# Block 2's mixers: the delta rule's chains as a third chain beside the RWKV column tiles

## The chip, the cores and the metric

The kernel runs on one core of a Trainium2 chip. The metric is the device time of one execution in microseconds (us). TensorE is called PE, VectorE DVE, ScalarE ACT, GpSimd POOL, and SyncE, which issues most DMAs, SP.

## What is computed

The program runs two blocks over 256 tokens of width 1024: a first block with its own mixers and a large expert layer, then a second block. Only the second block's mixing sublayer is touched. It projects the normalised input by `w_in`, splits the columns into a part for a gated delta rule (4 heads of 128), a part for RWKV-7 (8 heads of 64) and two gates, runs both recurrences in both directions over the sequence, and merges them:

```python
def gated_delta_chunked(q, k, v, g, beta, s0):
    ...
    gc = jnp.cumsum(g, axis=-1)
    a_mat = jnp.eye(CHUNK_2, dtype=jnp.float32) + lower
    sol = lax.linalg.triangular_solve(a_mat, rhs, left_side=True, lower=True, unit_diagonal=True)
    ...
    def step(s, inp):
        u_c, w_c, qk_c, qd_c, kd_c, ge_c = inp
        v_new = u_c - jnp.einsum('...ck,...kv->...cv', w_c, s)
        o_c = jnp.einsum('...ck,...kv->...cv', qd_c, s) + jnp.einsum('...ij,...jv->...iv', qk_c, v_new)
        s = s * ge_c[..., None, None] + jnp.einsum('...ck,...cv->...kv', kd_c, v_new)
        return s, o_c

def rwkv7_scan(r, w, k, v, a, b, s0):
    def step(s, inp):
        r_t, w_t, k_t, v_t, a_t, b_t = inp
        sa = jnp.einsum('...vk,...k->...v', s, a_t)
        s = s * w_t[..., None, :] + sa[..., :, None] * b_t[..., None, :] + v_t[..., :, None] * k_t[..., None, :]
        return s, jnp.einsum('...vk,...k->...v', s, r_t)

def merge_branches(gates, o_a, o_b, w_o_a, w_o_b, w_out):
    g_a, g_b = jnp.split(gates, 2, axis=-1)
    y = jax.nn.sigmoid(g_a) * (o_a @ w_o_a) + jax.nn.sigmoid(g_b) * (o_b @ w_o_b)
    return y @ w_out
```

## The kernel before

**RWKV.** The 512 channels are cut into four column tiles j of two heads each. A tile has a front, two backs and an output. `rwkv_front` makes, for each direction, the scaled operands and eight products `rmt` (L1648) that DVE and ACT evacuate into masks and transposes. `rwkv_back` is one chain per direction: an inverse (`mixed_inverse`: eight small tiled products `r0ic` or `r1ic` of L1172, then `ib` and `iy` of L1200, each of which needs the evacuated one before) and then four recurrence steps over chunks, each with the products L1681 (state by key), L1696 (inverse by residual) and L1703 (update), with an ACT or DVE evacuation between them; L1711 and L1688 add into the output. `rwkv_out` normalises (`ryt`, L1747, and `rgb`, L1752). The two directions go step by step in turn, with PSUM banks of their own (tags `pa` and `pc`), in `in_turn`.

**The delta rule.** It has four chains: two head pairs hp by two directions d. A chain takes the products of its head pair (`gdn_products`), a decay mask (`grb`, then DVE and ACT work on `gdec` and `gN`), an inverse with the prefix `gi`, and two recurrence steps (`gp`). It is written behind all RWKV tiles, in `gdn`: the two chains of hp 0 one after the other, those of hp 1 in step with each other from a second pool X.

**Work in queues.** Products that wait for nothing but their weights stand in two queues of generators. `waiting[0]` holds the next RWKV tile's preparation, `ahead(j+1)`: its projections (36 steps with the small ones), then `rn`, `rvb` and `rbw` (L1563, L1572, L1587) on the one bank of tag `pd`. `waiting[1]` holds the projections of head pair 1, the gate `gz` (L1856) and 16 early merge gates `early_gate` (eight `pc` products of L1110 each). `fill` takes a few steps from them behind a product of direction 0's chain. How many, by kind of product, is in `HOPS`: its entry 2 is for the inverse, 3 to 5 for the recurrence (queue 0, queue 1), and before also 6 and 7 for the delta rule.

**What sets the order.** The written order is not the order on the engines: a static scheduler puts each engine's instructions in a row when the program is built, and may move a chain's products ahead of ones written earlier. Memory pools are reused by tile, so a load may wait for the last reader of the tile that lay there before. `merge` (L1891) loads `w_o_b` in two halves on SP; ACT (L290) and DVE (L291) split each in two before the products `mo` (L300) may start.

Of the kernel before, what the change touches and what calls it, by code (L numbers as in the profile page):

```python
# [57 lines left out]

HOPS = 4, 1, (3, 1), (2, 1), (2, 1), (2, 1), (0, 4), (0, 4)
LBANKS = dict(pa=2, pc=2, pd=1, pb=2, pe=1)  # L60
# [80 lines left out]
def drain(steps):  # L141
    for _ in steps:
        pass


def run(steps):

    while True:
        try:
            next(steps)  # L150
        except StopIteration as end:
            return end.value
# [11 lines left out]
class Net:  # L164
# [796 lines left out]
    def ctx_pre(self):  # L961
# [6 lines left out]
        with tc.tile_pool(name="CW", bufs=2, reuse_waits="tile") as CW, tc.tile_pool(name="C", bufs=1, reuse_waits="tile") as C:  # L968
# [22 lines left out]
            with tc.tile_pool(name="CG", bufs=1, reuse_waits="tile") as G:  # L991
                gates = yield from self.gdn_gates(G, uT)
                for hp in range(2):
                    qkv = []
                    yield from self.gdn_in(G, uT, False, hp, load, qkv)
                    x = yield from self.gdn_products(G, qkv, False)
                    for d in range(2):
                        yield from self.gdn_dir(G, d, False, 2 * hp, gates, x, self.SA, False, None)
            with tc.tile_pool(name="CR", bufs=1, reuse_waits="tile") as R:
# [259 lines left out]

    def gdn(self, W, gates, ins, S, o, X):  # L1260


        for hp in range(2):
            x = run(self.gdn_products(W, ins[hp], True))
            args = 2 * hp, gates, x, S, True, o
            if hp == 0:
                for d in range(2):
                    drain(self.gdn_dir(W, d, False, *args))
            else:

                for _ in zip(self.gdn_dir(W, 0, True, *args), self.gdn_dir(X, 1, True, *args)):
                    pass

# [66 lines left out]

    def gdn_dir(self, W, d, both, h0, gates, x, S, lat, o):

        nc = self.nc
# [5 lines left out]
        c0 = 4 * d + h0  # L1349
        hop = (lambda *steps: (lambda ins: self.fill(ins, *steps))) if both and d == 0 else lambda *steps: (lambda ins: None)  # L1350
        rb = b4("grb")
# [12 lines left out]
        nc.scalar.activation(dec, dec, AF.Exp)  # L1364
        if not lat:
            yield
        N = W.tile([P, 2, 2, P], F32, name="gN")
# [14 lines left out]
        u4 = lambda ap: ap.rearrange("p t h c -> p (t h) c")  # L1382
        yield from self.mixed_inverse(W, u4(N), 4, d, u4(Y), 7, "gi", hop(*HOPS[6]))
        sl = S[d][:, h0:h0 + 2, :]
        for step in range(2):
# [3 lines left out]
            for h in range(2):  # L1389
                ins = nc.tensor.matmul(p1[:, h, :], kd[:, t, h, :], sl[:, h, :], start=True, stop=True)  # L1390
            hop(*HOPS[7])(ins)
            if not lat:
                yield
            r = W.tile([P, 2, P], F32, name="gr")
            nc.vector.tensor_sub(r, vN[:, t], p1)
            p2 = half("gp2")
            for h in range(2):
                ins = nc.tensor.matmul(p2[:, h, :], Y[:, t, h, :], r[:, h, :], start=True, stop=True)
            hop(*HOPS[7])(ins)
            if not lat:  # L1400
                yield
            vn = W.tile([P, 2, P], F32, name="gvn")
            nc.vector.tensor_mul(vn, p2, be[:, t, c0:c0 + 2].unsqueeze(2).to_broadcast([P, 2, P]))
            if lat:
                p3 = half("gp3")
                for h in range(2):
                    nc.tensor.matmul(p3[:, h, :], qd[:, t, h, :], sl[:, h, :], start=True, stop=False)
                    nc.tensor.matmul(p3[:, h, :], qk[:, t, h, :], vn[:, h, :], start=False, stop=True)
                ov = o[:, t, h0 * P:(h0 + 2) * P].rearrange("p (h c) -> p h c", h=2)
                if (step if both else d) == 0:  # L1410
                    nc.scalar.copy(ov, p3)
                else:
                    nc.vector.tensor_add(ov, ov, p3)
# [9 lines left out]
    def rwkv(self, W, F, uT, S, lat, load, tags, start=None):  # L1423
# [90 lines left out]
        self.waiting[0].append((tags[2], gate()))  # L1514
        start()
        for j in range(4):
# [6 lines left out]
            bo = self.rwkv_bonus(W, j, x, fr)  # L1523
            ys = self.in_turn(tags, [self.rwkv_back(j, d, x, fr[d], env) for d in range(2)])
            self.advance(self.waiting[0], 999)
# [235 lines left out]
    def lat(self):  # L1761
        tc, nc, I = self.tc, self.nc, self.I
        h = self.acc
        with ExitStack() as outer:
            L = outer.enter_context(tc.tile_pool(name="L", bufs=1, reuse_waits="tile"))
            early = [L.tile([P, KD, 256], F32, name=f"early{i}", tag=f"exp{i}") for i in range(2)]
            with self.phase(**LBANKS):
# [30 lines left out]
                self.ob = tail[:, 2, :].rearrange("p (j t) -> p j t", j=4)  # L1798
                with tc.tile_pool(name="R", bufs=1, reuse_waits="tile") as R, tc.tile_pool(name="G", bufs=1, reuse_waits="tile") as G, ExitStack() as mix:
                    slots = [self.wslot() for _ in range(3)]  # L1800
# [8 lines left out]
                    def start():  # L1809
# [5 lines left out]
                        others += [self.early_gate(j, loads[2], uT, early) for j in range(16)]  # L1815
                        self.waiting[1].extend(("pe", gen) for gen in others)

                    self.waiting = [], []
                    with tc.tile_pool(name="RF", bufs=1, reuse_waits="tile") as RF:
                        run(self.rwkv(R, RF, uT, self.SB, True, loads[0], ("pa", "pc", "pd"), start))  # L1820
                    slots[2].extend(part[:g])
                    X = mix.enter_context(tc.tile_pool(name="X", bufs=1, reuse_waits="tile"))
                    self.ptag = "pb"
                    self.gdn(G, self.gates, qkv, self.SA, go, X)
                    self.gdn_out(G, sz, go, oa)
# [477 lines left out]
```

## Time and profile before

| | us |
|---|---|
| median of 3 runs | 2464.67 (2458.88 to 2468.92) |
| the profiled execution | 2459.26 |
| its span | 2457.4 |
| block 2's mixers in it, first `afT` to first `mo` | 1676.57 to 2112.49 |
| mean granted PE clock, share of full speed | 0.97 |

PE is busy for 2280.8 of 2457.4 us, but a busy PE is not one at full speed: the granted clock falls to half in some stretches of the mixers. To read a stretch, take two things from its row: the time in which PE was not busy, and the busy time multiplied by what the clock lacked. Together they are what the stretch lost against a PE that always had work at full clock.

### The profile page before, as it was taken

Reading aid. Unit: us, or ns where it says so; the run is one execution under the profiler, and the core shown is the slowest. Engines: PE = TensorE matmul, PEld = TensorE weight load, DVE = VectorE, ACT = ScalarE, POOL = GpSimd, SP = SyncE. Lnnn points to the kernel's source line nnn. Section 1 sums busy time; section 2 is a strip of 40 time slices with the busy share of each in tenths; the row PEclk is TensorE's granted clock in tenths of the full one; section 3 lists DMA queues with packets and bytes.
Section 4 is the critical chain, followed back from the end, with each engine's and each line's share of the span. In section 5 each row is a group of like instructions: output and inputs, shape, how many; then the busy total and the mean of one; then the engine's idle time right before and its main releaser. Section 6 shows DMA issues by size and latency. Waiting matters only on the chain. (4 is left out here: it accounts for less than half of the span.)

```text
span 2457.4 us, 45180 instructions
## 1 busy us (share of the span) xinstructions
PE 2280.8 (93%) x18736; PEld 1238.1 (50%) x18736; DVE 979.8 (40%) x2419; ACT 652.7 (27%) x1652; POOL 353.7 (14%) x627
## 2 busy tenths in 40 slices
PE   7989799999999999899999999987989989989997
PEld 6756433444444443333343333325867868865554
DVE  7735311223233133232222232215576663545545
ACT  5414111211211222111122121104444433422222
POOL 3101000000000111011011011003253431300000
PEclk9989899999999999999999999998979989999999
DMA  7637999999999999999999999994211104689995
GB/s 257 213 115 262 356 395 402 402 407 406 398 400 395 366 391 405 406 408 405 406 406 404 406 407 408 406 398 115 79 39 47 52 22 145 202 278 366 366 368 181
DMA packets 318816, 755.06 MB, mean 307 GB/s; under 512 B 12944, under 2 KB 158016, under 8 KB 315536
## 3 DMA queue, kind: packets, MB, share of 16 engines
q1 hardware_dynamic: 317104, 747.67, 81.2%
q0 software_dynamic: 1504, 4.46, 0.5%
q8 instruction: 150, 2.46, 0.4%
q14 instruction: 58, 0.48, 0.1%
HBM read 751.03 MB, written 1.05 MB: 306 GB/s over the span
## 5 line engine op out<-in xcount | busy, mean ns | idle before, releaser
L909 PE MATMUL gu<-w,xs 128*64 128x512 f32 (+1 forms) x3072 | 677.7, 569 | 22.8 <-DMA w<-in_w_up 18.6
L909 PEld LDWEIGHTS gu<-w,xs 128*64 128x64 f32 x3072 | 197.1, 137 | 326.5 <-issue 257.4
L941 PE MATMUL dn<-w,hT 128*64 128x512 f32 x1408 | 336.3, 602 | 21.4 <-DMA w<-in_w_down 20.7
L1110 PE MATMUL pc<-luT,w 128*128 128x256 f32 x688 | 177.2, 399 | 2.2 <-DMA w<-in_w_in 1.5
L941 PEld LDWEIGHTS dn<-w,hT 128*64 128x64 f32 x1408 | 88.4, 136 | 176.6 <-issue 118.2
L1110 PEld LDWEIGHTS pc<-luT,w 128*128 128x128 f32 x688 | 127.3, 195 | 19.5 <-issue 1.5
L2159 PE MATMUL egu<-w,exs 128*64 128x256 f32 x1024 | 123.2, 383 | 0.0
L2159 PEld LDWEIGHTS egu<-w,exs 128*64 128x64 f32 x1024 | 74.6, 136 | 39.4 <-issue 6.9
L1692 POOL TENSOR_SCALAR rsw<-rSU,rwc 64x64 f32<-64x64 f32 x112 | 39.6, 354 | 379.1 <-DVE rSU L1708 368.9
L919 DVE TENSOR_TENSOR hid<-hid,gu 128x512 f32<-128x512 f32 (+1 forms) x48 | 30.9, 643 | 123.4 <-ACT hid L307 123.2
L920 DVE TENSOR_TENSOR hid<-hid,gu 128x512 f32<-128x512 f32 (+1 forms) x48 | 30.8, 642 | 120.4 <-PE gu L909 120.3
L1110 PE MATMUL pc<-cuT,w 128*128 128x256 f32 x288 | 71.1, 391 | 0.0
L305 ACT ACTIVATE hid<-gu 128x512 f32<-128x512 f32 (+1 forms) x48 | 26.9, 560 | 163.6 <-PE gu L909 163.4
L2186 PE MATMUL edn<-w,ehT 128*64 128x512 f32 x256 | 67.7, 597 | 0.7 <-ACT ehT L322 0.5
L1110 PEld LDWEIGHTS pc<-cuT,w 128*128 128x128 f32 x288 | 52.1, 190 | 30.8 <-issue 20.4
L291 DVE TENSOR_TENSOR wp<-w,wp 128x1024 fp32r<-128x1024 f32 (+1 forms) x44 | 57.8, 1332 | 24.2 <-ACT wp L290 24.2
L1700 DVE COPY rSU<-rp 64x64 f32<-64x64 f32 x64 | 13.5, 214 | 134.5 <-PE rp L1696 134.2
L300 PE MATMUL pj<-uTh,wp 128*128 128x272 f32 x320 | 66.0, 299 | 0.0
L1648 PE MATMUL rmt<-rT,rBK 128*128 128x128 f32 (+1 forms) x256 | 50.9, 340 | 15.3 <-DVE rT L1635 7.3
L290 ACT CAST wp<-w 128x1024 fp32r<-128x1024 f32 (+1 forms) x48 | 55.0, 1187 | 29.8 <-DMA w<-in_w_in 17.8
L1193 DVE TENSOR_TENSOR r0iB<-r0iB,r0ic 128x128 f32<-128x128 f32 x48 | 13.6, 284 | 118.5 <-PE r0ic L1172 107.2
L958 DVE SCALAR_TENSOR_TENSOR acc<-sc,aff,acc 128x512 f32<-128x512 f32 x64 | 43.7, 744 | 37.9 <-PE sc L956 37.7
(675 smaller groups left out, 3514.5 us busy)
## 6 DMA issues: line engine op xcount, KB each, us to landing
w<-in_w_down SPq DMA_DIRECT2D x176, 1024.0 KB, 16.5
w<-in_w_gate SPq DMA_DIRECT2D x128, 1024.0 KB, 17.6
w<-in_w_up SPq DMA_DIRECT2D x128, 1024.0 KB, 18.1
w<-in_w_gate SPq DMA_DIRECT2D x64, 768.0 KB, 15.8
w<-in_w_up SPq DMA_DIRECT2D x64, 768.0 KB, 14.9
w<-in_moe_w_gate SPq DMA_DIRECT2D x32, 1024.0 KB, 13.3
w<-in_moe_w_up SPq DMA_DIRECT2D x32, 1024.0 KB, 12.3
w<-in_moe_w_down SPq DMA_DIRECT2D x32, 1024.0 KB, 11.3
```

The lines of the kernel that those rows point to most:

```text
L290: self.nc.scalar.copy(hi, src)
L291: (eng or self.nc.vector).tensor_sub(lo, src, hi)
L300: self.nc.tensor.matmul(out, a[x], b[y], start=(i == 0 and x + y == 0), stop=(i == n - 1 and x == 1))
L909: ins = nc.tensor.matmul(b[h * 64:(h + 1) * 64, :w], xs[:, k, :], ws(k, slice(h * w, (h + 1) * w)), start=(k == 0), stop=(k == KD - 1))
L919: nc.vector.tensor_mul(hid, hid, gu[0][:, :w])
L941: ins = nc.tensor.matmul(dn[0][dc * 64:(dc + 1) * 64], hT[:, j, h * 64:(h + 1) * 64], wd(h * nf + j, slice(dc * 512, (dc + 1) * 512)), sta ...
L958: nc.vector.scalar_tensor_tensor(dst, b, self.aff[:, t + 1, e:e + 1], dst, op0=ALU.mult, op1=ALU.add)
L1110: self.nc.tensor.matmul(b, w(k), uT[:, k, :], start=(k == 0), stop=(k == KD - 1))
L1648: ins = nc.tensor.matmul(b[:, i], BK[:, c0 + i, h:h + 2, :], T[:, h, c0 + i, :, :], start=True, stop=True)
L1692: nc.gpsimd.tensor_scalar(sw[r], SU[r, h, c, :], wc[r, c:c + 1], 0.0, op0=ALU.mult, op1=ALU.add)
L2159: nc.tensor.matmul(b[64 * i:64 * i + 64, x * 256:x * 256 + 256], xs[:, k, i, :], w[i](k), start=(k == 0), stop=(k == KD - 1))
L2186: nc.tensor.matmul(b[64 * i:64 * i + 64, :], hT[:, j, 64 * i:64 * i + 64], wd[i](j, cs), start=(j == 0), stop=(j == 1))
```

## The change

The delta rule's chain number j runs as a third generator of `in_turn` beside RWKV tile j (tag `pb`), so `gdn`, its pool X and its own fills go. `third(j)` first pushes queue 1 until head pair 1's projections are there (j = 2). `HOPS[0]` = 10 steps of queue 1 run ahead of the first tile; the inverse's fill goes from (3, 1) to (2, 2), the recurrence's from (2, 1) to (1, 2). `gdn_dir` now gives way at every step; whether its output is copied or added hangs on d alone. The number of instructions stays: 18736 matmul records before, and no product is added or taken away.

```diff
-HOPS = 4, 1, (3, 1), (2, 1), (2, 1), (2, 1), (0, 4), (0, 4)
+HOPS = 10, 1, (2, 2), (1, 2), (1, 2), (1, 2)
...
-    def gdn(self, W, gates, ins, S, o, X):
-        for hp in range(2):
-            x = run(self.gdn_products(W, ins[hp], True))
-            args = 2 * hp, gates, x, S, True, o
-            if hp == 0:
-                for d in range(2):
-                    drain(self.gdn_dir(W, d, False, *args))
-            else:
-                for _ in zip(self.gdn_dir(W, 0, True, *args), self.gdn_dir(X, 1, True, *args)):
-                    pass
+    def gdn_turn(self, W, j, gates, qkv, S, o, held):
+        hp, d = divmod(j, 2)
+        if d == 0:
+            held[:] = [(yield from self.gdn_products(W, qkv[hp], True))]
+        yield from self.gdn_dir(W, d, 2 * hp, gates, held[0], S, True, o)
...
-        start()
+        third = start()
+        self.advance(self.waiting[1], HOPS[0])
         for j in range(4):
...
-            ys = self.in_turn(tags, [self.rwkv_back(j, d, x, fr[d], env) for d in range(2)])
+            ys = self.in_turn((*tags[:2], "pb"), [*(self.rwkv_back(j, d, x, fr[d], env) for d in range(2)), third(j)])
...
+                        held = []
+                        def third(j):
+                            while j == 2 and len(qkv[1]) < 3:
+                                self.advance(self.waiting[1], 1)
+                            return self.gdn_turn(G, j, self.gates, qkv, self.SA, go, held)
+                        return third
...
-                    X = mix.enter_context(tc.tile_pool(name="X", bufs=1, reuse_waits="tile"))
                     self.ptag = "pb"
-                    self.gdn(G, self.gates, qkv, self.SA, go, X)
                     self.gdn_out(G, sz, go, oa)
                     self.advance(self.waiting[1], 999)
```

**Place 1, PE, the recurrence of tile 0.** Before, two RWKV chains (`rp`) follow each other here without a queued product:

```order
L1688 MATMUL rp_12842<-rSU_12131,rT_11752 64x64 x2
L1696 MATMUL rp_12861<-rP_12854,rY_12222 64x64 x2
L1681 MATMUL rp_12851<-rSU_12177,rT_11753 64x64 x2
L1711 MATMUL rp_12842<-rSU_12131,rMR_12141 64x64
L1688 MATMUL rp_12851<-rSU_12177,rT_11753 64x64 x2
L1696 MATMUL rp_12872<-rP_12865,rY_12258 64x64 x2
```

After, in the same recurrence (lines are 10 lower), projections `pc`, gate products `gz` and a delta chain's inverse stand between the steps:

```order
L1693 MATMUL rp_13145<-rSU_12158,rKt_12167 64x64 x2
L1110 MATMUL pc<-luT,w 128x256
L1851 MATMUL gz<-w,luT 128x128 x4
L1701 MATMUL rp_13121<-rSU_12158,rMR_12168 64x64
L1200 MATMUL gib<-giZ,giN 128x128 x4
L1701 MATMUL rp_13132<-rSU_12201,rMR_12211 64x64
```

The queued products and the delta chain have moved in among the steps.

**Place 2, PE, from tile 0 to tile 1.** Before, tile 1's preparation (`rn`, `rvb`, `rbw`) stands at the first steps of tile 0's recurrence:

```order
L1696 MATMUL rp_12693<-rP_12686,rY_12222 64x64 x2
L1563 MATMUL rn<-rsq,stab 128x256
L1110 MATMUL pc<-luT,w 128x256
L1354 MATMUL grb<-ctab,gg 128x128 x2
L1688 MATMUL rp_12683<-rSU_12177,rT_11753 64x64 x2
```

After, it ends behind the recurrence, with products of the delta chain (`gp`) alone between, then tile 0's output and tile 1's front:

```order
L1577 MATMUL rbw<-rlo_11702,rlora 128x256
L1577 MATMUL rbw<-rlo_11703,rlora 128x256
L1396 MATMUL gp_13268<-gvn,gdec 128x128
L1395 MATMUL gp_13268<-SA_3013,ger 128x128
L1396 MATMUL gp_13268<-gvn,gdec 128x128
L1347 MATMUL grb<-stab,gg 128x128 x4
L1737 MATMUL ryt<-ctab,rys_12918 64x64 x8
L1742 MATMUL rgb<-rsg,rg_11767 128x256
L1638 MATMUL rmt<-rT_11752,rBK_13328 128x192 x2
```

The preparation has moved behind the recurrence, and between it and the front that needs it stand only these products.

**Place 3, PE, the end of the mixers.** Before, tile 3's `ryt` and `rgb` stand amid the delta rule's last inverses, some 50 rows ahead of `mo`:

```order
L1747 MATMUL ryt<-ctab,rys_15198 64x64 x8
L1200 MATMUL gib<-giZ,giN 128x128 x4
L1200 MATMUL giy<-gY,giB 128x128 x4
L1110 MATMUL pc<-luT,w 128x256 x4
L1752 MATMUL rgb<-rsg,rg_14008 128x256
```

After, RWKV's last step is followed by sixteen queued products, the delta rule's output `got`, then `ryt`, `rgb` and `mo`:

```order
L1678 MATMUL rp_16584<-rSU_15724,rT_11753 64x64 x2
L1686 MATMUL rp_16605<-rP_16601,rY_15806 64x64 x2
L1110 MATMUL pc<-luT,w 128x256 x8
L1701 MATMUL rp_16584<-rSU_15724,rMR_15734 64x64 x2
L1872 MATMUL got<-ctab,tail 128x128 x3
L1110 MATMUL pc<-luT,w 128x256 x8
L1872 MATMUL got<-ctab,tail 128x128 x3
L1737 MATMUL ryt<-ctab,rys_16353 64x64 x8
L1872 MATMUL got<-ctab,tail 128x128 x2
L1742 MATMUL rgb<-rsg,rg_14666 128x256
L300 MATMUL mo<-mob,wp 128x256 x96
```

The mixers now end with RWKV's output. The two loads of `w_o_b` take memory whose last readers are the RWKV products L1678 and L1686 shown here, so they are issued behind them; before, their waits were for RWKV tiles read earlier.

## Rows read from the trace of the kernel before

**Rows 1.** The page's first line.

```profile
span 2457.4 us, 45180 instructions
```

**Rows 2.** Busy by stretch: window, length, PE, PEld, DVE, ACT, POOL, PEclk, DMA, GB/s.

```profile
1677.00:1720.00 43.00, 36.53 (x193) 32.89 (x191) 23.86 (x69) 21.00 (x60) 20.31 (x44) 0.86 0.31 83
1720.00:1782.00 62.00, 61.56 (x773) 50.80 (x773) 32.74 (x90) 28.52 (x81) 14.28 (x26) 0.97 0.29 78
1782.00:1818.00 36.00, 27.64 (x360) 21.08 (x359) 27.66 (x77) 20.15 (x67) 18.73 (x31) 0.76 0.18 49
1818.00:1865.00 47.00, 45.16 (x790) 34.92 (x789) 26.98 (x89) 16.16 (x50) 17.68 (x38) 0.85 0.16 42
1865.00:1898.00 33.00, 29.94 (x261) 23.51 (x260) 27.09 (x76) 19.24 (x61) 15.80 (x24) 0.90 0.16 47
1898.00:1941.00 43.00, 40.82 (x926) 34.36 (x925) 25.83 (x85) 13.70 (x48) 17.21 (x38) 0.92 0.17 45
1941.00:1970.00 29.00, 28.63 (x317) 24.64 (x316) 20.66 (x60) 16.52 (x54) 11.63 (x19) 1.00 0.18 50
1970.00:2000.00 30.00, 26.68 (x403) 21.43 (x404) 24.58 (x81) 13.81 (x46) 17.14 (x30) 0.89 0.07 19
2000.00:2061.00 61.00, 53.57 (x1080) 41.03 (x1080) 25.93 (x77) 19.08 (x66) 12.26 (x22) 0.94 0.21 54
2061.00:2104.00 43.00, 41.55 (x256) 36.70 (x251) 17.20 (x35) 18.77 (x50) 4.52 (x9) 1.00 0.48 151
```

**Rows 3.** Groups of PE by form in 1677 to 2113: busy, mean ns, idle before.

```profile
L1110 PE MATMUL pc<-luT,w 128*128 128x256 f32 x688 | 177.2, 399 | 2.2 <-DMA w<-in_w_in 1.5 <-DVE tail L1860 0.7
L1648 PE MATMUL rmt<-rT,rBK 128*128 128x192 f32 x128 | 32.5, 393 | 7.9 <-ACT rT L1637 4.4 <-ACT rKt L1655 3.5
```

**Rows 4.** The same view as rows 2, in slices of 10 us.

```profile
1710.00:1720.00 10.00, 6.46 (x23) 5.99 (x23) 9.76 (x31) 3.33 (x10) 4.79 (x7) 0.51 0.01 4
1790.00:1800.00 10.00, 4.67 (x76) 3.42 (x75) 9.64 (x27) 7.74 (x26) 7.98 (x12) 0.78 0.05 13
1800.00:1810.00 10.00, 7.48 (x122) 5.54 (x114) 9.23 (x26) 4.00 (x15) 6.71 (x12) 0.50 0.01 2
```

**Rows 5.** PE's waits in 1677 to 2113: total us, times, longest.

```profile
PE rp L1711 <- DVE rSU L1700: 5.9, 6, 2.3
PE rp L1681 <- DVE rSU L1708: 5.4, 4, 2.1
PE r1ic L1172 <- DVE r1iB L1193: 4.1, 1, 4.1
```

**Rows 6.** Timeline of PE around tile 0's front: start, us, instruction, wait before it.

```profile
1698.79 0.60 PE L1563 MATMUL rn<-rsq,stab 128*128 128x256 f32 x2
1699.22 1.03 PE L1587 MATMUL rbw<-rlo,rlora 128*128 128x256 f32 x4
1701.83 1.11 PE L1587 MATMUL rbw<-rlo,rlora 128*128 128x256 f32 x4
1711.47 2.92 PE L1648 MATMUL rmt<-rT,rBK 128*128 128x192 f32 x8 [4.41 <-ACT rT L1637]
1716.46 1.62 PE L1648 MATMUL rmt<-rT,rBK 128*128 128x192 f32 x4 [2.06 <-ACT rKt L1655]
```

**Rows 7.** Timelines of the mixers' end, SP's loads, then PE, DVE, ACT.

```profile
L1891 SPq DMA_DIRECT2D w<-in_w_o_b x2: 458/490/522, 2061.2 to 2061.8; - x2
...
2054.60 0.34 PE L1711 MATMUL rp<-rSU,rMR 128*64 128x64 f32 x4
2112.49 1.77 PE L300 MATMUL mo<-mob,wp 128*128 128x256 f32 x13
...
2065.57 0.60 DVE L1753 TENSOR_TENSOR tail<-rys,rgb 128x256 f32<-128x256 f32 x1 [0.89 <-PE rgb L1752]
2075.76 2.29 DVE L291 TENSOR_TENSOR wp<-w,wp 128x2048 fp32r<-128x2048 f32 x1
...
2099.94 1.30 ACT L290 CAST mob<-tail 128x256 fp32r<-128x256 f32 x4
2105.23 1.89 ACT L290 CAST wp<-w 128x2048 fp32r<-128x2048 f32 x1
```

## What the change was expected to do

> **What bounds the kernel now.** The change touches only block 2's mixers, 1677 to 2113 us of a span of 2457.4 [rows 1]; what follows them waits for their end, so their length is the whole effect. I read first the table of busy times by stretch, which shows what PE lost in each; then PE's waits, to see which engine ended them; then the slices of 10 us, to see whether that engine was itself full; and last the timelines around the two places where the new order looks worst.
>
> From the table [rows 2], take for each stretch the time in which PE was not busy, and its busy time multiplied by the clock it lacked. For 1782 to 1818 that is 36.0 − 27.64 = 8.4, and 27.64 × (1 − 0.76) = 6.6, together 15.0 us. The ten stretches in turn lost 11.6, 2.3, 15.0, 8.6, 6.1, 5.5, 0.4, 6.3, 10.6 and 1.5 us; the last 9 us, not in the table, lost 0.6. The 11.6 lie ahead of tile 0's first products, where the new order on PE is the old one: they stay. The other 56.9 us are all that an even feed of PE could win; the work itself, 2113 − 1720 − 56.9 = 336 us at full clock, has the same instructions before and after.
>
> The reader should see the contrast in [rows 2]. Where queued projections stand between the steps (1720 to 1782, 1941 to 1970, 2061 to 2104) PE lost 2.3 + 0.4 + 1.5 = 4.2 us in 134. Where they are missing it lost 15.0 in 36. What PE waits for in the bad stretches is mostly DVE: its copies and updates of the RWKV state (5.9 and 5.4 us) and one step of an inverse (4.1) [rows 5]. In 1790 to 1810 DVE was busy for 9.64 and 9.23 of 10 us, and the granted clock went 0.78, 0.50 [rows 4], that is half its time and more at the lower of its levels, 1.2 instead of 2.4 GHz, after PE had worked for under half of a slice. So a missing filler costs twice, first as idle time and then as clock.
>
> By the Trainium skill (TensorE: Matmul & The Clock Gate, "What's actually happening") the clock granted follows how busy PE has lately been; the 0.50 behind the slice with 4.67 us of work agrees, and by that rule a stretch that is fed wins its clock too, as the sum below assumes with or without the rule.
>
> **The change part by part.** *Nothing is removed.* Of PE, DVE, ACT and POOL the work is the same; pool X's removal and the choice of copy or add by direction move one DVE or ACT instruction of about 0.4 us each and cost nothing where PE has products queued. What moves is the delta rule's chains, from behind RWKV to a place beside each tile, and the queued products, out of the delta rule's tail into the tiles. I counted PE's instructions of the new order between its marks, priced each kind by its mean (a `pc` product is two records, 177.2 us for 688, 0.52 us for the two [rows 3]) and scaled the sum to the 336 us above. Then each stretch gets the rate of loss of the stretch of [rows 2] that it is most like:
>
> 1. Tile 0, from its front to the end of its recurrence, some 102 us of work, with `pc` or `gz` behind each step: the rate of 1720 to 1782, 2.3 on 60, gives 3.8 (bounds 3, and 8, a third of what the rate of 1818 to 1865, 8.6 on 38, would give).
> 2. Tile 0 to tile 1. The recurrence has 10 × 2 + 11 × 1 = 31 places for queue 0, and `ahead(1)` has 36 steps, so `rn`, `rvb` and `rbw` now come last and one behind another on one bank. In tile 0's own front the first `rbw` started at 1699.22 and the first `rmt` at 1711.47, 12.25 us later, and from `rn` to the last `rbw` took 1701.83 − 1698.79 = 3.0 us [rows 6]. With the last projection's own evacuation, some 1.8 us as I estimate it from ACT's and DVE's 0.4 us steps, that makes 17.1 us in which PE has about 8.8 us of products: 8.3 idle. Then the front's evacuations follow: a second wait of 2.06 us stood there in tile 0 [rows 6], and its slice from 1710 lost 10 − 6.46 × 0.51 = 6.7 us in all [rows 4]. I take 5 of these, so 13.5 (bounds 9.6, where the gate's products hide part of the evacuations, and 18). In the old order the same place was the worst stretch of all, 15.0 us.
> 3. Tile 1: its inverse is fed, 45 us of work at (2.3 + 0.4) / 91, 1.4 (bounds 1 and 6). The last two thirds of its recurrence have hardly a queued product, 21 us of work; the nearest stretches are 1898 to 1941 (5.5 on 37) and 1782 to 1818 (15.0 on 21). I take 6, nearer to the first, since a delta chain's products now lie between (bounds 3 and 15).
> 4. Tile 2: front with pairs of `pc`, 22 us of work, like 1970 to 2000 (6.3 on 24): 5 (0.5 to 8). Inverse and first steps, 34 us, fed: 1.0 (0.5 to 5). The rest, 20 us with some `pc`, between 1941 to 1970 and 1898 to 1941: 2.5 (0.3 to 9).
> 5. Tile 3: front, 18 us, like 1865 to 1898 (6.1 on 27): 4 (2 to 8). The rest, 44 us with two `pc` at a time: 1.3 (0.6 to 6).
> 6. The end. Before, the last RWKV product stood at 2054.60 and `mo` at 2112.49, 58 us later, and `w_o_b` had been loaded since 2061 [rows 7]: all of RWKV's output was hidden by the delta rule. Now it is the end. From the last RWKV product to the finished output took 2065.57 + 0.60 − 2054.60 = 11.6 us. Behind it come the casts of it (1.30), ACT's cast of the late `w_o_b` (1.89) and DVE's part of its split (2.29) [rows 7]: 17.1 us, under which PE has sixteen `pc` (8.2) and some 2.2 us of small products. 17.1 − 10.4 = 6.7, taken as 7 (bounds 5, if the casts of the load go first, and 11, if the load lands late).
>
> The losses add to 3.8 + 13.5 + 1.4 + 6 + 5 + 1.0 + 2.5 + 4 + 1.3 + 7 = 45.5, against 56.9: a gain of 11.4 us, 2459.3 − 11.4 = 2447.9 against the profiled execution. That one lies near the lower end of the three runs, 5.4 under their median; a new median lies within such a spread, so I add 2 and forecast 2450.
>
> **The rivals.** *A, the even feed cures nearly all.* If the third chain and the pairs of `pc` cover the fronts too, the losses come to the lower bounds, 3 + 9.6 + 1 + 3 + 0.5 + 0.5 + 0.3 + 2 + 0.6 + 5 = 25.5: 31 us gained, 2430. For it speaks that the fed stretches lost 3% only [rows 2]; against it, that DVE, not PE, was full in the bad ones [rows 4].
>
> *B, nothing is gained.* The built order before already had the delta rule's first chains and `grb` between tile 0's steps, so "beside" is not new; what was won inside tiles 1 to 3 is handed back at points 2 and 6, which together are 20.5 us. That gives 2458 to 2468; the mark is fed tiles, and two holes of 13 us and 7 us or more.
>
> *C, DVE's queue becomes the bound, slower.* Each tile now carries a delta chain's mask and inverse on DVE next to two RWKV chains, and the small state updates stand behind them in the queue. If the recurrences of tiles 1 to 3 then lose what 1782 to 1818 lost, 15.0 us each, in place of 6, 2.5 and (as a part of 1.3) about 0.8, the losses rise by 9 + 12.5 + 14.2 = 35.7, to 81: 24 us slower, 2484. It decides where DVE is busy for more than 9 of 10 us through a recurrence, as at 1790 [rows 4]. Against it: DVE's ten stretches hold 252.5 us of work in 427 [rows 2], 59%, so there is room if the work is spread.
>
> For C also speaks a rule of the Trainium skill (Trainium Kernel Development and Optimization, "Best Practices"): tiling on TensorE makes the products faster, and not the evacuation of PSUM; the small tiled products of the inverses are such, and by that rule a third chain adds to a queue that packing did not shorten. The full DVE beside a half-idle PE at 1790 agrees with it, the fed stretches do not.
>
> **How the numbers follow.** Forecast 0.43 (2441 to 2459), A 0.15 (2424 to 2441), B 0.22 (2458 to 2468), C 0.20 (2468 to 2495). A measurement of this kernel tells about 0.5% from no change, 12.3 us, so against the median of 2464.7 faster ends at 2452 and slower begins at 2477. Of the forecast's case I put 0.30 under 2452 and 0.13 over it: faster 0.30 + 0.15 = 0.45, same 0.13 + 0.22 = 0.35, slower 0.20. The range for 8 in 10 leaves out the lower half of A and the upper half of C: 2431 to 2482.
>
> **What would show it.** In the profile after, the mixers' length against 436 us. For point 1: the stretch that was 1782 to 1818 at full clock, with no waits for the RWKV state over 1 us. For point 2: a wait of PE at tile 1's first `rmt` of several us, for ACT's `rT`, and a low clock behind it. For point 3: waits for DVE's `rSU` in tile 1's recurrence. For point 6: SP's loads of `w_o_b` within about 20 us of `mo`, and PE idle or slow there for about 7 us. The prediction is wrong if DVE is full through whole tiles (C), or if the fronts of tiles 2 and 3 show no loss (A), or if the first column of projections, which the ten steps of `HOPS[0]` draw forward, moves tile 0's start by more than 3 us.

## The result, and the profile after

The changed kernel takes 2482.1 us (median of 7 runs, 2477.75 to 2484.11), the kernel before 2458.88 beside it: a ratio of 1.0084 (1.0069 to 1.0099). By that ratio it is 20.6 us slower; the two medians lie 23.2 apart. The forecast was 2450, in a range of 2431 to 2482, and the sign was missed.

Two lengths tell where the time went: the mixers, from the first `afT` of block 2 to the first `mo`, and the merge, from there to the first expert product `exg`. The span grew by 19.5 us: mixers 435.9 to 443.8, merge 67.0 to 77.4, and 1.1 and 0.2 ahead of and behind these. So about half of the loss lies behind the mixers, where the prediction had put nothing at all.

The stretches of the mixers after, in the columns of [rows 2]:

```profile
span 2476.9 us, 45161 instructions
...
1678.00:1721.00 43.00, 36.54 (x190) 32.75 (x188) 23.20 (x66) 21.05 (x60) 20.43 (x44) 0.86 0.31 83
1721.00:1770.00 49.00, 48.61 (x573) 40.66 (x573) 27.68 (x83) 24.57 (x71) 12.54 (x20) 0.95 0.28 77
1770.00:1790.00 20.00, 13.61 (x219) 10.95 (x218) 14.24 (x31) 8.44 (x22) 6.65 (x9) 0.74 0.20 54
1790.00:1838.00 48.00, 47.64 (x587) 38.33 (x586) 24.79 (x67) 20.30 (x66) 12.49 (x31) 1.00 0.29 78
1838.00:1870.00 32.00, 21.83 (x207) 18.48 (x208) 30.37 (x89) 14.48 (x45) 19.95 (x27) 0.79 0.03 7
1870.00:1930.00 60.00, 58.02 (x1055) 48.43 (x1054) 25.97 (x76) 23.07 (x71) 12.91 (x32) 1.00 0.21 56
1930.00:1960.00 30.00, 23.88 (x246) 19.08 (x248) 26.14 (x83) 15.07 (x47) 17.88 (x30) 0.94 0.09 24
1960.00:2020.00 60.00, 55.59 (x1015) 43.17 (x1001) 22.98 (x67) 21.84 (x69) 14.24 (x31) 1.00 0.18 47
2020.00:2051.00 31.00, 26.37 (x300) 20.77 (x300) 28.53 (x95) 15.26 (x52) 19.06 (x33) 0.94 0.13 35
2051.00:2106.00 55.00, 48.32 (x950) 37.87 (x949) 21.46 (x62) 16.14 (x56) 10.76 (x25) 0.97 0.20 52
2106.00:2122.00 16.00, 11.12 (x75) 8.76 (x74) 11.11 (x33) 11.72 (x38) 2.03 (x3) 0.90 0.47 166
```

Read as before, idle time plus busy time by the missing clock, they lost 11.6, 2.8, 9.9, 0.4, 14.8, 2.0, 7.6, 4.4, 6.2, 8.1 and 6.0 us: 62.2 behind the first, against 56.9. That is 5.3 of the 7.9 us by which the mixers grew; the rest is PE's work itself, 401 − 62.2 = 338.8 us at full clock, against 336. In part the feed did get even: tile 0's recurrence (1790 to 1838) runs at full clock with 0.4 us lost, where 1782 to 1818 had lost 15.0. But three places are nearly full on DVE instead: 1838 to 1870 (30.4 of 32 us), 1930 to 1960 (26.1 of 30) and 2020 to 2051 (28.5 of 31). These are the fronts of tiles 1 to 3, with the start of a delta chain beside each. (Tile 0's own front, as before, has 4.4 of the 9.8 us in the next list.) PE's waits in the mixers, total, times, longest:

```profile
PE rmt L1638 <- ACT rT L1627: 9.8, 2, 5.4
PE rmt L1638 <- ACT rKt L1645: 7.2, 6, 2.1
PE r0ib L1200 <- DVE r0iZ L1204: 6.4, 1, 6.4
PE pc L1110 <- DMA w<-in_w_in: 6.4, 8, 2.8
```

Of [rows 5] hardly anything is left (0.2 us for `rSU`); the waits are now mostly at the fronts and in tile 0's inverse. Tile 0 meets the start of its own chain, on DVE and PE in order of time:

```profile
1771.89 0.86 DVE L1354 SCALAR_TENSOR_TENSOR gdec<-grb,ggc,stab 128x128 f32<-128x128 f32 x3
1774.16 2.86 DVE L1364 SCALAR_TENSOR_TENSOR gN<-gkq,gbe,gdec 128x128 f32<-128x128 f32 x4 [0.29 <-ACT gdec L1357]
1777.73 1.96 DVE L1177 COPY giB<-gN 32x128 f32<-32x128 f32 x2
1781.29 0.66 DVE L1204 STREAM_TRANSPOSE r0iZ<-rY 128x512 f32<-128x512 f32 x1
...
1782.00 2.08 PE L1200 MATMUL r0ib<-r0iZ,r0iN 128*128 128x128 f32 x8 [6.39 <-DVE r0iZ L1204]
```

The chain's mask stands in DVE's queue ahead of the transpose that the RWKV inverse needs, and PE waits 6.4 us. Not all of this is DVE's own work. POOL, in the same stretch:

```profile
1773.68 1.31 POOL L1368 TENSOR_TENSOR gkd<-gx,ger 128x512 f32<-128x512 f32 x1 [4.49 <-ACT ger L1356]
1775.08 1.26 POOL L1371 TENSOR_TENSOR ger<-gx,ger 128x512 f32<-128x512 f32 x1
1777.09 1.84 POOL L1207 TENSOR_TENSOR giN<-gN,stab 128x512 f32<-128x512 f32 x1 [0.75 <-DVE gN L1364]
```

Of the four `gN` above, two took 0.34 us each and two 0.99 and 1.42; these end at 1775.15 and 1776.49, just behind POOL's `gkd` (1775.00) and `ger` (1776.34). The first copy `giB` took 1.28 us, against 0.22 for the shortest of its kind, and ends at 1779.01, behind `giN` (1778.94). Setting each DVE instruction of the mixers against the faster fifth of its kind gives an estimate of this lengthening: 2.6 us in 1770 to 1790, 7.5 of the 30.4 busy us in 1838 to 1870, and 26.4 in the whole mixers, where the kernel before had 25.9. It has not grown, then; part of it lies where PE waits, before (5.2 us in 1782 to 1818) as after. No run moved POOL's work in the mixers, so what it costs there is open.

In the merge the weights come late. Timelines of SP, then PE, DVE and POOL:

```profile
2106.70 2.06 SPq L1886 DMA_DIRECT2D w<-in_w_o_b  x2
2123.76 2.57 SPq L1886 DMA_DIRECT2D w<-in_w_o_a  x2
2129.51 5.97 SPq L1886 DMA_DIRECT2D w<-in_w_out  x4
...
2121.46 2.08 PE L300 MATMUL mo<-mob,wp 128*128 128x256 f32 x8 [4.30 <-ACT wp L290]
2152.51 4.01 PE L300 MATMUL mw<-wp 128*128 128x512 f32 x8 [3.39 <-ACT wp L290]
2160.01 10.11 PE L300 MATMUL mw<-wp 128*128 128x512 f32 x37 [3.50 <-DVE wp L291]
...
2143.08 4.25 DVE L291 TENSOR_TENSOR wp<-early,wp 128x256 fp32r<-128x256 f32 x1 [0.20 <-ACT wp L290]
2147.26 4.76 DVE L1920 TENSOR_TENSOR early<-early,early 128x256 f32<-128x256 f32 x1
2152.38 0.42 DVE L1920 TENSOR_TENSOR early<-early,early 128x256 f32<-128x256 f32 x1
...
2137.65 14.09 POOL L291 TENSOR_TENSOR wp<-w,wp 128x2048 fp32r<-128x2048 f32 x3 [19.94 <-ACT wp L290]
```

`w_o_b` is issued at 2106.7, 45 us later than in [rows 7]. `w_o_a` and `w_out` then wait for buffers: SP waited 13.5 us there for DVE's splits, 11.7 the longest. While POOL splits `w_out`, from 2137.65 to 2151.74, a DVE instruction that takes 0.42 us elsewhere (the third DVE row) takes 4.25 and 4.76.

### The profile page after: what moved, and what is told of

Same layout as the page of the kernel before. It is cut to its first block, busy times and chain, and to the rows that moved or that the text cites. A ratio compares the mean times of both kernels' runs of the same rounds, so it can differ in the third digit from the quotient of the medians.

```text
span 2476.9 us, 45161 instructions
## 1 busy us (share of the span) xinstructions
PE 2274.8 (92%) x18736; PEld 1232.3 (50%) x18736; DVE 992.3 (40%) x2419; ACT 653.2 (26%) x1652; POOL 352.2 (14%) x627
## 5 line engine op out<-in xcount | busy, mean ns | idle before, releaser
L919 DVE TENSOR_TENSOR hid<-hid,gu 128x512 f32<-128x512 f32 (+1 forms) x48 | 30.8, 642 | 124.9 <-ACT hid L307 124.7
L920 DVE TENSOR_TENSOR hid<-hid,gu 128x512 f32<-128x512 f32 (+1 forms) x48 | 30.8, 641 | 120.1 <-PE gu L909 119.9
L1110 PEld LDWEIGHTS pc<-cuT,w 128*128 128x128 f32 x288 | 52.0, 189 | 30.8 <-issue 20.4
L1638 PEld LDWEIGHTS rmt<-rT,rBK 128*128 128x128 f32 x256 | 41.0, 211 | 39.8 <-issue 13.3
## 6 DMA issues: line engine op xcount, KB each, us to landing
w<-in_w_up SPq DMA_DIRECT2D x64, 768.0 KB, 14.8
w<-in_moe_w_gate SPq DMA_DIRECT2D x32, 1024.0 KB, 13.3
```

Source lines behind the costliest of these rows:

```text
L919: nc.vector.tensor_mul(hid, hid, gu[0][:, :w])
L1110: self.nc.tensor.matmul(b, w(k), uT[:, k, :], start=(k == 0), stop=(k == KD - 1))
L1638: ins = nc.tensor.matmul(b[:, i], BK[:, c0 + i, h:h + 2, :], T[:, h, c0 + i, :, :], start=True, stop=True)
```

## The experiments

All times stand against runs of the kernel before on the same chip; the interval is in brackets, and a gain or loss in us is taken from the ratios. Mixers and merge come from one profiled execution each. For the mixers that is rough: where the edit hardly touches them they still came out at 435.9, 430.7 and 437.5 (before, e7, e16), and at 443.8 and 446.9 (after, e8). By these the growth is between 6 and 16 us, and a difference of 5 us between two rows alone shows little. The merge is steadier: 67.0 twice (before, e13), and 64.4 or 64.5 in e3, e5, e12 and e14.

| run | mixers | merge | ratio to before |
|---|---|---|---|
| before | 435.9 | 67.0 | 1 |
| after | 443.8 | 77.4 | 1.0084 (1.0069 to 1.0099) |
| e1 early `w_o_b` | 450.5 | 71.5 | 1.0048 (1.0030 to 1.0066) |
| e2 delay | 434.9 | 75.4 | 1.0005 (0.9992 to 1.0018) |
| e3 old fills | 447.7 | 64.4 | 1.0028 (1.0011 to 1.0046) |
| e4 before, new fills | 455.2 | 71.8 | 1.0085 (1.0056 to 1.0114) |
| e5 delay, old fills | 443.0 | 64.5 | 1.0021 (1.0006 to 1.0035) |
| e6 delay, buffers | 428.3 | 78.2 | 1.0036 (1.0015 to 1.0057) |
| e7 before, late loads | 430.7 | 79.5 | 1.0028 (1.0010 to 1.0046) |
| e8 split on DVE | 446.9 | 73.9 | 1.0056 (1.0038 to 1.0073) |
| e9 delay, buffers, early `w_o_b` | 429.2 | 77.4 | 1.0004 (0.9991 to 1.0017) |
| e10 as e9, split on DVE | 428.8 | 71.3 | 0.9982 (0.9968 to 0.9997) |
| e11 buffers | 438.7 | 77.9 | 1.0043 (1.0026 to 1.0061) |
| e12 delay, old fills, buffers | 428.0 | 64.5 | 0.9977 (0.9959 to 0.9996) |
| e13 before, buffers | 443.8 | 67.0 | 1.0037 (1.0023 to 1.0051) |
| e14 old fills, buffers | 445.4 | 64.4 | 1.0014 (1.0001 to 1.0028) |
| e15 as e12, split on DVE | 429.4 | 64.5 | 0.9986 (0.9967 to 1.0004) |
| e16 before, split on DVE | 437.5 | 64.4 | 0.9989 (0.9972 to 1.0006) |

**e1, early loads.** Tile 3's turn loads `w_o_b` into idle weight buffers:

```diff
+                            if j == 3:
+                                for i in range(2):
+                                    t = whole[i][:, :2048].rearrange("p (k c) -> p k c", k=4)
+                                    nc.sync.dma_start(t, I["w_o_b_2"][...])
...
-                    slots[2].extend(part[:g])
+                    slots[2].extend(part[4:g])
...
-            rr, re, rd, self.Q, E = ...
+            self.Q, E, rd, re, rr = ...
```

> The changed kernel, with w_o_b's two halves loaded at the start of tile 3's turn into two weight buffers that stand idle by then, and the merge's buffers laid where no RWKV tile is read late. Everything before the mixers' end stays. Theory L (the late loads of the merge's weights cost most of the loss): the first mo product comes within 2 us of the last got or rgb instead of 4.3 us later, w_o_a is issued right behind the last w_in load, and the stretch from the first mo to the first router transpose falls from 48.5 to about 39 us: 12 to 15 us faster than the changed kernel, a span of about 2463. Theory D (the tiles, where DVE is full, cost most of it): under 5 us.

Measured: 8.9 us faster than the changed kernel. The merge shrank by 5.9, but the mixers grew by 6.7 in their profile: PE's waits for `w_in` rose from 6.4 to 11.2 us, since the early gates have fewer buffers. The splits of `w_o_b`, which now stand ahead of the last tile's output on ACT and DVE, may be the rest; that is not shown. `w_out` was still issued at 2129. Theory L got its direction and about two thirds of its size.

**e2, delay.** Each delta chain first gives way six times:

```diff
     def gdn_turn(self, W, j, gates, qkv, S, o, held):
+        for _ in range(6):
+            yield
         hp, d = divmod(j, 2)
```

> The changed kernel, with each delta chain given six turns of delay, so that its mask and products start inside the tile's inverse and not beside the tile's front. Theory D (the start of a delta chain and a tile's front stand in one DVE queue): the three stretches around the fronts of tiles 1 to 3, which lost 14.8, 7.6 and 6.2 us, lose 8 to 12 us less in all, and PE's waits for ACT's rT and rKt (17 us in the mixers) halve; the mixers get 6 to 10 us shorter, unless the last delta chain then ends behind RWKV. Theory L: the mixers' length changes by under 3 us and the merge stays at 48 us.

Measured: 19.4 us faster than the changed kernel, level with the kernel before. The mixers became 8.9 us shorter, and PE's waits for `rT` and `rKt` fell from 17.0 to 7.4. The gain came elsewhere than expected, though: at tile 0's inverse, not in the hole behind it. The two stretches:

```profile
1770.00:1790.00 20.00, 19.83 (x224) 16.92 (x223) 16.59 (x37) 10.25 (x28) 7.05 (x10) 1.00 0.25 66
1820.00:1860.00 40.00, 27.57 (x298) 24.50 (x295) 33.58 (x102) 18.50 (x57) 21.99 (x33) 0.79 0.09 23
```

The first lost 9.9 us without the delay and 0.2 with it. The second, from tile 0 to tile 1, lost 12.43 + 5.8 = 18.2: the start of the next chain, with an 8.1 us wait of PE for DVE's `giB`, still falls there. The spans of the two profiled executions differ by only 13.4 us: besides the mixers these are 2.0 of merge, since `w_o_b` went out at 2086.8, and 2.3 ahead of the mixers, which no step of the change explains.

**e3, old fills with the third chain.**

```diff
-HOPS = 10, 1, (2, 2), (1, 2), (1, 2), (1, 2)
+HOPS = 10, 1, (3, 1), (2, 1), (2, 1), (2, 1)
```

> The changed kernel with the old fills, (3, 1) in the inverse and (2, 1) in the recurrence, ten steps ahead as in the change. The next tile's preparation then ends inside the recurrence, which leaves it room before the next front. If the new split of the queues makes the hole between tiles 0 and 1 (14.8 us lost there), that stretch loses 6 to 9 us and the kernel is 5 to 8 us faster than the changed one. If the hole comes from the full DVE alone, it stays over 12 us and the time within 3 us.

Measured: 13.8 us faster than the changed kernel, 7 slower than before. The hole between tiles 0 and 1 went. The last of the preparation (`rbw`) and tile 1's first `rmt`, in the changed kernel and then in e3, with two stretches of e3:

```profile
1839.92 1.13 PE L1577 MATMUL rbw<-rlo,rlora 128*128 128x256 f32 x4 [0.26 <-ACT ric L305]
1850.88 1.62 PE L1638 MATMUL rmt<-rT,rBK 128*128 128x192 f32 x4 [5.40 <-ACT rT L1627]
...
1802.14 1.03 PE L1577 MATMUL rbw<-rlo,rlora 128*128 128x256 f32 x4
1826.11 1.65 PE L1638 MATMUL rmt<-rT,rBK 128*128 128x192 f32 x4
...
1826.00:1842.00 16.00, 15.76 (x97) 13.79 (x96) 11.44 (x45) 5.08 (x20) 5.94 (x15) 0.87 0.00 1
1800.00:1826.00 26.00, 22.46 (x244) 16.42 (x242) 19.05 (x52) 15.50 (x49) 12.64 (x19) 0.69 0.09 27
```

Tile 1's front (1826 to 1842) lost 0.24 + 2.05 = 2.3 us, and DVE had room, 11.4 of 16. The end of tile 0's recurrence, 1800 to 1826, lost 3.54 + 7.0 = 10.5, as 1782 to 1818 had before. This holds beyond e3: from tile 0's last recurrence product to the last `rmt` of tile 1's front, the nine kernels of the table with the new fills lost 7.8 to 20.0 us, and the nine with the old fills 0.1 to 3.1. Over the whole mixers e3 won nothing by it (447.7): its gain is the merge, 13.0 us shorter. With fewer steps of queue 1 taken inside the tiles, early gates are left for the end, and SP issues the merge's weights between their loads:

```profile
2087.18 1.07 SPq L1886 DMA_DIRECT2D w<-in_w_o_b  x2
2091.04 4.56 SPq L253 DMA_DIRECT2D w<-in_w_in  x2
2099.22 3.43 SPq L1886 DMA_DIRECT2D w<-in_w_o_a  x2
```

**e4, the new fills in the kernel before.**

```diff
-HOPS = 4, 1, (3, 1), (2, 1), (2, 1), (2, 1), (0, 4), (0, 4)
+HOPS = 4, 1, (2, 2), (1, 2), (1, 2), (1, 2), (0, 4), (0, 4)
```

> The kernel before with the new fills alone, (2, 2) and (1, 2), the delta rule behind RWKV as it was. If the even spread of the queued products is what costs, it is 5 to 12 us slower than before, with the hole between tiles 0 and 1 in it. If the third chain and the late loads cost, it is within 5 us of before, and its merge weights are still loaded some 50 us ahead of the first mo.

Measured: 20.9 us slower than before, as much as the whole change. The delta rule's tail, which before lost 1.5 us in 43 [rows 2], ran out of queued products at 2095.6:

```profile
2060.00:2128.00 68.00, 55.92 (x602) 45.29 (x603) 29.15 (x77) 24.00 (x73) 9.29 (x19) 0.86 0.24 76
...
2110.00:2120.00 10.00, 8.61 (x35) 7.72 (x36) 2.52 (x7) 2.39 (x9) 0.00 (x0) 0.50 0.49 182
2120.00:2130.00 10.00, 6.00 (x24) 4.69 (x24) 6.24 (x18) 6.02 (x21) 3.14 (x8) 0.50 0.09 15
```

It lost 12.1 + 7.8 = 19.9 us, with the clock at half at the end. The hole ahead of tile 1's front is there too (10.1 us), and the merge is 4.8 us longer. The spread of the products alone is enough for the loss; in the changed kernel the third chain takes the tail away, and the loss sits at the fronts and in the merge.

**e5, delay and old fills.** Both edits above.

> The changed kernel with both: each delta chain delayed by six turns, and the old fills (3, 1) and (2, 1). From the runs so far the delay took 9 us off the mixers with the new fills and the old fills took 13 us off the merge. If the two causes (starts of chains on DVE beside a front; queued products and loads of weights used up before the end) are separate, mixers about 437 us and merge about 36, together 473, the same as the kernel before within 3 us or up to 5 faster. If they are one cause, the sum stays over 479.

Measured: mixers 443.0, merge 64.5; 1.0021. The merge's gain stayed, the mixers' did not: with the old fills the delay is worth 4.7 us in the mixers, not 8.9. Both edits took the same hole, so they need not add; but the difference is also within what two profiles of the same mixers differ by.

**e6, delay and even buffers.** Six buffers for three streams of weights: RWKV's, head pair 1's with the gate's, the early gates'.

```diff
-LPARTS = (3, 5)
+LPARTS = (2, 4)
```

> The run with the delay of six turns and the new fills, with the six weight buffers dealt 2, 2, 2 to the three streams in place of 3, 2, 1, so that the early gates' products no longer share one buffer. If PE's waits for w_in loads in the tiles (7.8 us there, 1.5 before) come from that one buffer, they fall under 2 us and the mixers are 4 to 6 us shorter. If the loads are late because SP's queue holds them, the waits stay.

Measured: no wait for `w_in` is left, and the mixers are the shortest so far, 428.3, 6.6 less than with the delay alone. The time rose all the same, to 1.0036: the merge took 78.2 and what follows 4 us more; the runs do not say why. Shorter mixers met weights that came no earlier (`w_o_b` at 2084.9, `w_o_a` at 2107.5).

**e7, the kernel before with late loads.** Only the order of the merge's buffers in memory:

```diff
-            rr, re, rd, self.Q, E = ...
+            self.Q, E, rd, re, rr = ...
```

> The kernel before with the merge's buffers laid elsewhere in memory, so that the loads of w_o_b are issued behind the last w_in load and no longer 25 us ahead of it; nothing else moves on PE ahead of mo. Theory L (a late start of the merge's loads is paid in the merge, whatever the tiles do): w_o_b is issued after 2086, w_o_a after 2100, the stretch from the first mo to the first router transpose grows from 38 to 43 us or more and the kernel is 5 to 10 us slower. If the merge has slack, the time stays within 2 us.

Measured: 7 us slower than before. `w_o_b` went out at 2102.5, and the merge grew by 12.5 us, more than the changed kernel's 10.4. The mixers were 5.2 shorter, and were so by tile 3's front, ahead of the casts that the edit moves out of them. The clock parts them: behind the same wait at tile 1's front (1.84 and 1.85 us) it was at half for the next 10 us in the kernel before, the first row, and full in e7, the second.

```profile
1830.00:1840.00 10.00, 10.00 (x208) 6.13 (x206) 7.26 (x22) 2.24 (x8) 4.91 (x7) 0.50 0.18 48
1830.00:1840.00 10.00, 7.82 (x255) 5.32 (x255) 9.30 (x34) 3.54 (x13) 5.57 (x8) 1.00 0.04 11
```

DVE and POOL in the merge of e7:

```profile
2131.60 0.41 DVE L1904 TENSOR_TENSOR early<-early,mo 128x256 f32<-128x256 f32 x1
2132.21 4.25 DVE L291 TENSOR_TENSOR wp<-early,wp 128x256 fp32r<-128x256 f32 x1 [0.20 <-ACT wp L290]
2136.38 4.78 DVE L1925 TENSOR_TENSOR early<-early,early 128x256 f32<-128x256 f32 x1
...
2126.78 14.10 POOL L291 TENSOR_TENSOR wp<-w,wp 128x2048 fp32r<-128x2048 f32 x3 [16.09 <-ACT wp L290]
```

POOL's three splits of 4.7 us end near 2131.5, 2136.2 and 2140.9; the two long DVE instructions end at 2136.46 and 2141.16, with the second and the third.

**e8, `w_out` split on DVE, in the changed kernel.**

```diff
-        wo = [parts(w, nc.gpsimd) for w in ws[:2]]
+        wo = [parts(w, nc.vector) for w in ws[:2]]
...
-                wo += [parts(w, nc.gpsimd) for w in ws[2:]]
+                wo += [parts(w, nc.vector) for w in ws[2:]]
```

> The changed kernel with w_out's four splits on DVE in place of POOL, 2.29 us each there against 4.7. In its merge single DVE instructions of 128x256 took 3.7 to 4.9 us instead of 0.42 while POOL split a half of w_out. If DVE waits there for POOL, those lengths vanish, DVE gets 9.2 us of work in their place, and the merge falls from 48.5 to 42 to 45 us. If the lengths have another cause, they stay and the merge is as long or longer.

Measured: no DVE instruction of 128x256 over 2.3 us is left in the merge, which falls by 3.5 us (48.5 to 43.2 up to the first router transpose); the kernel is 6.9 us faster than the changed one, though its profiled span is only 0.9 shorter, with mixers 3.1 longer. DVE did wait there for POOL.

**e9 and e10, delay, buffers and early `w_o_b`; then the split on DVE.**

> Delay of six turns, buffers dealt 2, 2, 2, the new fills, and w_o_b's halves loaded at tile 3 into the two buffer pairs that are idle by then, as in the early-load run. If the mixers' loss (chains beside fronts, one buffer) and the merge's loss (late loads) are separate, mixers about 430 us as with the delay and the buffers, merge about 41, together 471, 3 us under the kernel before's 474 and 21 under the changed kernel. If taking the casts into the mixers gives back on DVE and ACT what the merge wins, the mixers are 435 or longer and the sum stays over 474.

> As the run before it, with w_out's four splits on DVE instead of POOL. If DVE's long instructions in the merge come from POOL's splits alone, the merge loses another 2 to 5 us, to 37 to 40; if DVE's own 9.2 us of splits stand in the merge's path instead, it is as long or longer. The mixers stay within 2 us of the run before it.

Measured: e9 kept the mixers short (429.2), but the merge stayed at 77.4: `w_o_a` now went out early (2080.7), but `w_out` at 2114.5, 8 us behind the first `mo`; before it had been 2 us ahead of it. e10 took 6.1 us off it and ended at 0.9982.

**e11 to e14, what the buffers do.** e11 is the changed kernel with the buffers 2, 2, 2; e12 adds delay and old fills; e13 is the kernel before with these buffers; e14 is e12 without the delay.

> The changed kernel with the six weight buffers dealt 2, 2, 2 alone, no delay. If the one buffer of the early gates costs by itself, PE's waits for w_in loads fall from 6.4 us to under 2 and the mixers from 443.8 to 438 to 441. If the buffers only pay together with the delay, since PE then waits for DVE at the fronts instead, the waits for loads fall and the mixers stay within 2 us of 443.8.

> Delay of six turns, the old fills, and buffers dealt 2, 2, 2: the run with delay and old fills had mixers of 443.0 and a merge of 35.5 us. If its waits for loads and for evacuations of the early gates (6 us) come from the buffers, the mixers fall to 437 to 439 and the sum to 473, level with the kernel before; else they stay at 443.

> The kernel before with the six weight buffers dealt 2, 2, 2 and nothing else. If the gain of the buffers (5.1 us in the mixers with the new fills, 15.0 with the delay and the old fills) needs the third chain, which draws the early gates into the tiles, the mixers stay within 3 us of 435.9, since waits for w_in were only 1.5 us there. If the one buffer cost the kernel before as much, the mixers fall by 5 us or more, and the buffers are no part of why the change was slower.

> The changed kernel with the old fills and buffers dealt 2, 2, 2, and no delay. With the delay this had mixers of 428.0 us. If the delay takes a cost of its own (chains starting beside a front), the mixers are 433 to 440 here; if the buffers alone were behind the 15 us, they are within 2 us of 428.

Measured: with the third chain the buffers take the waits for `w_in` away (6.4 us to 0 in e11), and e11 is 10 us faster than the changed kernel, with mixers 5.1 shorter. The gain is not where the waits had been: behind tile 1's front e11 lost 36.9 us, the changed kernel 34.0. It is in tile 0's inverse and recurrence, 3.7 us lost for 11.7. In the kernel before the same buffers cost 9 us (e13). There the first `rmt` comes 42.6 us behind the first `afT`, in place of 34.9, with sixteen more `pc` records ahead of it; RWKV's stream has a buffer less, but no wait of PE for `w_in` shows. So the buffers are part of what the changed kernel lost, and no general gain; how they act is not shown. e14 against e12 parts the delay from the buffers: mixers 445.4 without it, 428.0 with it. e12 is the best version by its ratio, 0.9977, about 6 us faster than the kernel before, at the edge of what can be told. Its weights leave SP early:

```profile
2066.09 1.09 SPq L1888 DMA_DIRECT2D w<-in_w_o_b  x2
2076.83 3.17 SPq L1888 DMA_DIRECT2D w<-in_w_o_a  x2
2089.12 16.61 SPq L1888 DMA_DIRECT2D w<-in_w_out  x4
```

**e15 and e16, the split on DVE where the loads are early.**

> Delay, old fills, buffers 2, 2, 2, and w_out's splits on DVE. In the run without the last part the merge's loads were early and the stretch from mo to the first expert product was 64.5 us with one long DVE instruction. If the splits on DVE only pay where the loads are late, the merge is the same within 2 us or longer, and the time too; if POOL's splits cost even here, 2 to 4 us less.

> The kernel before with w_out's splits on DVE. One DVE instruction of 4.8 us stands in its merge, behind POOL's last split. If that wait is on the path, the merge (67.0 us from mo to the first expert product) falls by 3 to 5 us and the kernel is 3 to 5 us faster; if DVE's own 9.2 us of splits take its place, no change.

Measured: in e15 the merge is 64.5 with or without it. In e16 it fell by 2.6 us; the time, 0.9989 (0.9972 to 1.0006), can't be told from no change. POOL's splits cost much only where the loads are late.

## Why the prediction was wrong

**What failed first** is a sentence ahead of the sum: "what follows them waits for their end, so their length is the whole effect". The merge grew by 10.4 us. Point 6 had the late `w_o_b` and sized the hole at the end well (7 forecast, 6.0 lost in 2106 to 2122), but stopped at the first `mo`. `w_o_a` takes the buffers that `w_o_b` leaves, and `w_out` those behind it, so the delay goes on for three loads and ends on POOL's splits. e7 shows this without any other part of the change: 12.5 us. Early loads take it away: the merge is 64.4 in e3, and 64.5 in e12.

**Point 1, a term of 3.8 us.** Tile 0 lost 2.8 + 9.9 + 0.4 = 13.1. The rate of 1720 to 1782 was taken for a stretch that gets something that one had not: the start of a chain on DVE. e2 moved it and the 9.9 went. The forecast read fed stretches as a property of PE's row; they were also stretches in which DVE was idle for 47, 29 and 60% of the time [rows 2].

**Point 2** came out at 14.8 for 13.5, with the wait at tile 1's first `rmt` (5.4 us, for ACT's `rT`) and the low clock behind it, as written. The reason given, a preparation that comes too late for lack of places in queue 0, held: `rbw` ended 4.6 us behind the recurrence, and with the old fills (e3) the preparation was early again and the front lost 2.3. What the point left out is that the loss does not vanish with the hole: in e3 10.5 us stood in tile 0's recurrence instead. DVE was busy for 30.4 of the 32 us, about a quarter of that being lengthening beside POOL by the estimate above. (In the sum, 8.3 and 5 add to 13.3.)

**Points 3 to 5.** Tile 1's inverse and recurrence lost 2.0 where 7.4 were set; its recurrence was fed well enough. Tile 2's front lost 7.6 for 5, its rest 4.4 for 3.5; tile 3's front 6.2 for 4, its rest 8.1 for 1.3. One missing term is the early gates' single weight buffer: drawn into the tiles, they waited for loads, 6.4 us in 8 waits against 1.5. The text ahead of the prediction says that queued products "wait for nothing but their weights", and the weights were not priced. These waits are 3.3 of the 4.4 us in tile 2's rest, but only 2.3 of the 8.1 in tile 3's. Another 3.9 there are three waits of PE ahead of `gic` and `r1ic` for which the profile shows no cause, so the step that failed is the rate taken for tile 3's rest, and most of its cause stays open.

**In sum** the prediction's terms came to 45.5 us of loss, and 62.2 were measured. These 16.7 and the merge's 10.4 make up most of the 30.8 us between the gain of 11.4 that was forecast and the 19.4 by which the profiled execution was slower. By point, measured less forecast, they are 9.3, 1.3, −5.4, 3.5, 9.0 and −1.0.

**The rivals.** C gave 2484 and the time is 2482, but C's mechanism was not seen: it wanted DVE full through the recurrences of tiles 1 to 3, and these lost 2.0 and 4.4 in tiles 1 and 2. DVE was full at a front, and half of the loss was outside. That C's number fits is chance. Of B's mark the holes were there, 14.8 and 6.0 us for 13 and 7, but not the fed tiles: tile 0 lost 13.1. A fell. The rule of the Trainium skill (Trainium Kernel Development and Optimization, "Best Practices") that TensorE tiling does not speed up PSUM evacuation was not what decided: where PE waited 6.4 us, DVE's queue held masks and copies that read SBUF (`gN`, `giB`).

**The fills** were counted as the gain. Alone they cost as much as the whole change (e4), because the products had been the cover of the tail. They also made the hole of point 2. Part of the mixers' loss stays unsettled: the effects of delay, fills and buffers do not add (the delay is worth 8.9 us with the new fills, 4.7 with the old, 17.4 with the old fills and even buffers, each from single profiles that may be 5 us off), and no run parts them further.

## What to carry to other kernels

Queued work has a place where it already hides something: before spreading it, find what it covers now, and what its weights' buffers and the order in which their loads are issued allow. A sum over a stage must go on to the next stage's loads, for an end that comes in another order moves their issue. When chains are put beside each other, lay their heavy starts apart on the engine that evacuates, here DVE, and look at that engine's busy time by slice, not by its mean, and at whether single instructions in it are longer than the same ones elsewhere. A loss that leaves one stretch must be looked for in its neighbours.

## What the runs showed of the hardware

A DVE subtraction or addition of 128x256 whose two inputs lie in SBUF took 0.42 us alone and 4.25 to 4.78 beside POOL's split, ending with it; an instruction of the same size with one input from PSUM (`early<-early,mo`) took 0.41 in the midst of it. The Trainium skill (SBUF — State Buffer, "SBUF: two separate sides") states this: GpSimd and a DVE instruction with two SBUF inputs share a port pair that one of them holds for its whole instruction. The traces of the changed kernel and of e7 agree, and with the splits on DVE (e8) the long instructions are gone. The masks and copies of the mixers, `gN` at 0.99 and 1.42 us for 0.34 and `giB` at 1.28 for 0.22, show the same lengthening beside POOL at tile 0.
